# Gated linear attention in a two-layer decoder trunk: one score product per level for both 128-token blocks, and a new order of the gate rows

## The chip, the cores and the metric

One core of a Trainium2 chip runs the whole program in one launch. The metric is device time in microseconds (us). The time of the kernel before is the median of three runs. TensorE does matrix products, VectorE (DVE) and ScalarE (ACT) elementwise work, GpSimd (POOL) simple elementwise work, SyncE (SP) issues the transfers.

## The reference, cut to what matters

A batch of one with 256 tokens, 16 learned meta tokens ahead of them (272 rows), width 2048, passes two layers: gated linear attention (GLA) and a squared-ReLU MLP, then sliding-window attention and another MLP. The change lies in the GLA:

```python
q, k, v, g, r = split(xn @ w_in)                       # 4 heads, 256 key columns each
gk = log_sigmoid(r @ w_gate_up + b_gate) / 16          # a decay per key column and token
# per chunk of 64 tokens:
b = cumsum(gk)                                         # within the chunk
decay = exp(where(causal, b_i - b_j, -inf))
attn[i, j] = sum_d q[i, d] * k[j, d] * decay[i, j, d]
o = attn @ v + (q * exp(b)) @ S
S = S * exp(b_last) + (k * exp(b_last - b))^T @ v
```

The decay lies inside the sum over d, so attn isn't one matrix product of q and k.

## The kernel before

Everything is held transposed: features on the 128 partitions, tokens along the free axis. All big products are f32 made of three passes of a rounded type: `split_weight` (L84) makes of every 128x1024 half of a weight a rounded `hi` on ScalarE (L87) and the remainder `lo` on VectorE (L89), and `passes` (L99) issues, for each of 8 pieces, hi x hi, hi x lo and lo x hi (L110 to L112). A product (`product`, L114) thus has two halves of 24 matmuls; each needs its hi, and from its third matmul on its lo. `hi` and `lo` have three buffers each, `raw` four or more. The Tile scheduler, which goes by estimates of its own, orders each engine's queue from the dependencies; only the prologue (L265) fixes the order of TensorE, ScalarE and VectorE by hand, and other ready instructions may still be put between.

The prologue makes the normed input, the gate's low-rank rows `rr` and the first four key products. Then come the other key products (L316), the gate rows (L326: a small matmul `ps_z`, then abs, exp and ln on ScalarE, a minimum, a subtraction and a scan on VectorE, which give the running sums of the log decay `B`), eight query products (L339, ending in L341) and sixteen value products (`v_tile`, L361: the product, a scaling L364, three transposes `pt`).

Between the value products run the scores, a generator of steps (`scores`, L385), once for each pair of heads. A chunk's causal square is cut into levels s = 32, 16, ..., 1: in each block of 2s tokens the second s attend to the first s, and with the reference point at the end of the first s the decay splits into two factors of which neither grows. Per level: two GpSimd subtractions `E` (L411, L412), one exponential (L414), a product with the keys in place (L416) and one with the queries into `QL` (L417), which holds only the second halves, 64 columns per 128-token block. Then for each of the two blocks, two heads and two column groups one product `ps_l`: keys of the block as weights (128 columns), 64 query columns moving. VectorE masks the result (L423) and adds it, strided, into the scores `AT` (L426). The diagonal has its own products `ps_d` (L403, L404). After the levels: `QE` and `KD` carry the decays between chunks (L430 to L438); `ps_c` (L446) links the two chunks of a block, `ps_x` one block to the other, `ps_m` the meta tokens. `mix` (L513) multiplies the scores with the values.

Of the kernel before, what the change touches and what calls it, by code (L numbers as in the profile page):

```python
# [62 lines left out]
def trunk(ctx: ExitStack, tc: tile.TileContext, a: dict, out: bass.AP):  # L63
# [138 lines left out]
    def load(name, shape):  # L202
        t = const.tile(shape, F32, name=name)
        nc.sync.dma_start(t, a[name])
        return t
# [7 lines left out]
    with ExitStack() as gla:  # L213
# [109 lines left out]
        nc.gpsimd.memset(reset[:, 0:1], 0.0)  # L323
        nc.gpsimd.memset(reset[:, NM:L:CH], 0.0)
        B = bp.tile([P, 8, L], F32, tag="B", name="B")
        for f in range(8):  # L326
            ps = aux.tile([P, 512], F32, tag="aux", name="ps_z")
            nc.tensor.matmul(ps[:, :L], wgs[:, f * P:(f + 1) * P], rr, start=True, stop=True)
            e = tp.tile([P, L], F32, tag="t1", bufs=4, name="ge")
            nc.scalar.activation(e, ps[:, :L], AF.Abs, bias=bg[:, f:f + 1])  # L330
            lz = tp.tile([P, L], F32, tag="t2", bufs=4, name="gl")
            nc.vector.tensor_scalar(lz, ps[:, :L], bg[:, f:f + 1], 0.0, ALU.add, ALU.min)
            nc.scalar.activation(e, e, AF.Exp, scale=-1.0)
            nc.scalar.activation(e, e, AF.Ln, bias=1.0)
            nc.vector.tensor_sub(lz, lz, e)
            nc.vector.tensor_tensor_scan(B[:, f], reset, lz, 0.0, ALU.mult, ALU.add)

        Q = bp.tile([P, 8, L], F32, tag="Q", name="Q")
        for m in range(8):  # L339
            ps, = product(a["w_in"][m], xs)  # L340
            nc.vector.scalar_tensor_tensor(Q[:, m], ps, QS, rs, ALU.mult, ALU.mult)  # L341
# [43 lines left out]
        def scores(hp):  # L385
# [7 lines left out]
            def head_products(dst, n, lhs, rhs):  # L393

                for g in range(G):
                    for c in range(2):
                        t = 2 * g + c
                        nc.tensor.matmul(dst(g), lhs(t), rhs(t), start=(c == 0), stop=(c == 1))

            ps = aux.tile([P, 512], F32, tag="aux", name="ps_d")  # L400
            for jt in range(2):
                js = slice(jt * P, (jt + 1) * P)
                head_products(lambda g: ps[:, (jt * G + g) * P:(jt * G + g + 1) * P], P, lambda t: Kx[:, t, js], lambda t: Qx[:, t, js])  # L403
            nc.vector.tensor_mul(A_.rearrange("p g j i -> p j g i"), ps.rearrange("p (j g i) -> p j g i", j=2, g=G), ident[:, None, None, :].broadcast_to([P, 2, G, P]))  # L404
            yield
            for li, s in enumerate(LEVELS):
                n = SEQ // (2 * s)
                v = lambda t: t.rearrange("p f (n two s) -> p f n two s", two=2, s=s)
                E = bp.tile([P, F, SEQ], F32, tag="E", bufs=2, name="E")
                ref = v(Bx)[:, :, :, 0, s - 1:s].broadcast_to([P, F, n, s])  # L410
# [4 lines left out]
                QL = bp.tile([P, F, P], F32, tag="QL", bufs=2, name="QL")  # L415
                nc.vector.tensor_mul(v(E)[:, :, :, 0, :], v(E)[:, :, :, 0, :], v(Kx)[:, :, :, 0, :])  # L416
                nc.vector.tensor_mul(QL.rearrange("p f (n s) -> p f n s", s=s), v(E)[:, :, :, 1, :], v(Qx)[:, :, :, 1, :])  # L417
                yield
                ps = aux.tile([P, 512], F32, tag="aux", name="ps_l")
                for jt in range(2):  # L420
                    head_products(lambda g: ps[:, (jt * G + g) * CH:(jt * G + g + 1) * CH], CH, lambda t: E[:, t, jt * P:(jt + 1) * P], lambda t: QL[:, t, jt * CH:(jt + 1) * CH])
                psm = bp.tile([P, 2 * G * CH], F32, tag="psm", bufs=2, name="psm")
                nc.vector.tensor_mul(psm.rearrange("p (g i) -> p g i", i=CH), ps[:, :2 * G * CH].rearrange("p (g i) -> p g i", i=CH), lmask[:, None, li, :].broadcast_to([P, 2 * G, CH]))  # L423
                for jt in range(2):
                    dst = A_[:, :, jt].rearrange("p g (n two s) -> p g n two s", two=2, s=s)[:, :, :, 1, :]
                    nc.vector.tensor_add(dst, dst, psm[:, jt * G * CH:(jt + 1) * G * CH].rearrange("p (g n s) -> p g n s", g=G, s=s))  # L426
                yield

            Bc = Bx.rearrange("p f (c s) -> p f c s", s=CH)
# [4 lines left out]
            nc.vector.tensor_sub(KD[:, :, NM:].rearrange("p f (c s) -> p f c s", s=CH), Bc[:, :, :, CH - 1:CH].broadcast_to([P, F, NC, CH]), Bc)  # L434
            nc.vector.tensor_sub(KD[:, :, :NM], B_[:, :, NM - 1:NM].broadcast_to([P, F, NM]), B_[:, :, :NM])
            yield
            nc.scalar.activation(KD, KD, AF.Exp, scale=GATE)
            nc.vector.tensor_mul(KD, KD, K_)  # L438
# [3 lines left out]
            yield  # L442

            ps = aux.tile([P, 512], F32, tag="aux", name="ps_c")
            for jt in range(2):
                head_products(lambda g: ps[:CH, (jt * G + g) * CH:(jt * G + g + 1) * CH], CH, lambda t: KDx[:, t, jt * P:jt * P + CH], lambda t: QE[:, t, jt * P + CH:(jt + 1) * P])  # L446
            for jt in range(2):
                nc.vector.tensor_copy(A_[:CH, :, jt, CH:], ps[:CH, jt * G * CH:(jt + 1) * G * CH].rearrange("p (g i) -> p g i", i=CH))
# [23 lines left out]
            for li, s in enumerate(MLEVELS):  # L472
                n = NM // (2 * s)
                v = lambda t: t.rearrange("p f (n two s) -> p f n two s", two=2, s=s)
                ref = v(Bm)[:, :, :, 0, s - 1:s].broadcast_to([P, F, n, s])
                kv5 = v(K5[:, :, li])
                nc.vector.tensor_sub(kv5[:, :, :, 0, :], ref, v(Bm)[:, :, :, 0, :])
# [419 lines left out]
```

## Time and profile before

| | us |
|---|---|
| median of three runs (2210.8 to 2212.07) | 2211.91 |
| the profiled execution | 2212.41 |
| its span, first to last instruction | 2210.6 |
| TensorE busy | 2189.8 |
| VectorE busy | 1362.0 |
| ScalarE busy | 1066.9 |
| GpSimd busy | 237.0 |

The profiled execution is 0.5 us above the median, and 1.8 us of it lie outside the span. In a row of a timeline stand the start, the busy time, the engine, the source line, what is written and read, the shape, the count, and in brackets how long the engine sat idle just before and what ended that. In rows that group instructions the first number is the sum of busy times in us and the second the mean of one in ns. Matmuls are pipelined: one of 128x272 is busy 0.29 us, while the next starts 0.125 us after it, so prices on TensorE are read from start to start. The query products end at 117 us, the value products run from there to 256 us, the MLP and the second layer fill the rest and aren't touched.

### The profile page before, as it was taken

Reading aid. Unit: us, or ns where it says so; the run is one execution under the profiler, and the core shown is the slowest. Engines: PE = TensorE matmul, PEld = TensorE weight load, DVE = VectorE, ACT = ScalarE, POOL = GpSimd, SP = SyncE. Lnnn points to the kernel's source line nnn. Section 1 sums busy time; section 2 is a strip of 40 time slices with the busy share of each in tenths; the row PEclk is TensorE's granted clock in tenths of the full one; section 3 lists DMA queues with packets and bytes.
Section 4 is the critical chain, followed back from the end, with each engine's and each line's share of the span. In section 5 each row is a group of like instructions: output and inputs, shape, how many; then the busy total and the mean of one; then the engine's idle time right before and its main releaser. Section 6 shows DMA issues by size and latency. Waiting matters only on the chain. (4 is left out here: it accounts for less than half of the span.)

```text
span 2210.6 us, 38682 instructions
## 1 busy us (share of the span) xinstructions
PE 2189.8 (99%) x15796; PEld 2079.0 (94%) x15796; DVE 1362.0 (62%) x1941; ACT 1066.9 (48%) x1672; POOL 237.0 (11%) x248
## 2 busy tenths in 40 slices
PE   9999999999999999999999999999999999999997
PEld 9999999999999999999999999988888888888886
DVE  6768676665445545544556666686656655656665
ACT  5544455444334434433444568655435534534543
POOL 0112143310000000000013121060000000000022
PEclk9999999999999999999999999999999999999999
DMA  6443445565555555555554554466555555555552
GB/s 226 161 136 118 133 157 164 173 214 177 172 178 175 172 177 176 173 177 176 172 178 156 164 181 141 134 217 195 189 190 191 187 190 189 189 190 191 189 184 94
DMA packets 107393, 383.80 MB, mean 174 GB/s; under 512 B 13136, under 2 KB 14160, under 8 KB 107216
## 3 DMA queue, kind: packets, MB, share of 16 engines
q1 hardware_dynamic: 105056, 378.34, 52.2%
q0 software_dynamic: 1152, 2.38, 0.4%
q8 instruction: 123, 2.02, 0.4%
q10 hardware_dynamic: 1008, 0.63, 0.1%
q14 instruction: 54, 0.44, 0.1%
HBM read 376.82 MB, written 2.10 MB: 171 GB/s over the span
## 5 line engine op out<-in xcount | busy, mean ns | idle before, releaser
L87 ACT CAST hi<-raw 128x1024 fp32r<-128x1024 f32 x711 | 745.2, 1049 | 1038.9 <-PE ps L111 571.9
L89 DVE TENSOR_TENSOR lo<-raw,hi 128x1024 fp32r<-128x1024 f32 x711 | 878.4, 1236 | 597.0 <-ACT hi L87 589.8
L112 PE MATMUL ps<-x,lo 128*128 128x272 f32 (+1 forms) x2112 | 609.6, 289 | 4.4 <-DVE lo L89 4.2
L110 PE MATMUL ps<-x,hi 128*128 128x272 f32 (+1 forms) x2112 | 610.6, 289 | 0.5 <-ACT hi L275 0.3
L111 PE MATMUL ps<-x,hi 128*128 128x272 f32 (+1 forms) x2112 | 608.4, 288 | 0.3 <-DVE x L151 0.2
L112 PEld LDWEIGHTS ps<-x,lo 128*128 128x128 f32 x2112 | 397.2, 188 | 6.0 <-DVE lo L89 5.3
L111 PEld LDWEIGHTS ps<-x,hi 128*128 128x128 f32 x2112 | 401.4, 190 | 1.0 <-DVE x L151 0.9
L110 PEld LDWEIGHTS ps<-x,hi 128*128 128x128 f32 x2112 | 397.7, 188 | 3.7 <-issue 0.7
L107 PE MATMUL ps<-x,hi 128*128 128x512 f32 x1024 | 357.1, 392 | 0.0
L107 PE MATMUL ps<-hid,hi 128*128 128x512 f32 x1024 | 356.6, 392 | 0.0
L110 PE MATMUL ps<-hid,hi 128*128 128x272 f32 x1024 | 295.4, 289 | 0.0
L112 PE MATMUL ps<-hid,lo 128*128 128x272 f32 x1024 | 295.4, 289 | 0.0
L111 PE MATMUL ps<-hid,hi 128*128 128x272 f32 x1024 | 294.9, 288 | 0.0
L108 PE MATMUL ps<-x,lo 128*128 128x256 f32 x1024 | 287.6, 281 | 0.0
L108 PE MATMUL ps<-hid,lo 128*128 128x256 f32 x1024 | 287.1, 281 | 0.0
L107 PEld LDWEIGHTS ps<-x,hi 128*128 128x128 f32 x1024 | 192.0, 188 | 42.9
L107 PEld LDWEIGHTS ps<-hid,hi 128*128 128x128 f32 x1024 | 191.8, 188 | 42.6
L111 PEld LDWEIGHTS ps<-hid,hi 128*128 128x128 f32 x1024 | 194.8, 190 | 0.0
L108 PEld LDWEIGHTS ps<-hid,lo 128*128 128x128 f32 x1024 | 193.2, 189 | 0.3
L108 PEld LDWEIGHTS ps<-x,lo 128*128 128x128 f32 x1024 | 193.2, 189 | 0.1
L110 PEld LDWEIGHTS ps<-hid,hi 128*128 128x128 f32 x1024 | 192.4, 188 | 0.0
L112 PEld LDWEIGHTS ps<-hid,lo 128*128 128x128 f32 x1024 | 192.4, 188 | 0.0
(218 smaller groups left out, 2063.6 us busy)
## 6 DMA issues: line engine op xcount, KB each, us to landing
raw<-in_w_up SPq DMA_DIRECT2D x256, 512.0 KB, 3.4
raw<-in_w_down SPq DMA_DIRECT2D x256, 512.0 KB, 3.4
raw<-in_w_in SPq DMA_DIRECT2D x95, 512.0 KB, 3.3
raw<-in_w_out_a SPq DMA_DIRECT2D x32, 512.0 KB, 3.3
raw<-in_w_q SPq DMA_DIRECT2D x32, 512.0 KB, 3.9
raw<-in_w_out_b SPq DMA_DIRECT2D x32, 512.0 KB, 3.3
raw<-in_w_kv SPq DMA_DIRECT2D x8, 512.0 KB, 3.3
sw<-qt POOLq DMA_DIRECT2D x32, 64.0 KB, 2.4
```

The lines of the kernel that those rows point to most:

```text
L87: nc.scalar.copy(hi, raw)
L89: nc.vector.tensor_sub(lo, raw, hi.bitcast(F32))
L107: nc.tensor.matmul(ps[:, :2 * n], wh, x.both, start=begin, stop=False)
L108: nc.tensor.matmul(ps[:, n:2 * n], wl, x.hi, start=False, stop=end)
L110: nc.tensor.matmul(ps[:, :n], wh, x.hi, start=begin, stop=False)
L111: nc.tensor.matmul(ps[:, :n], wh, x.lo, start=False, stop=False)
L112: nc.tensor.matmul(ps[:, :n], wl, x.hi, start=False, stop=end)
```

## The change

**Levels.** Both blocks share one product: keys of the first block and queries of the second are the weights, queries of the first and keys of the second move, all 128 columns wide. A tile `W` holds for the first block its decayed keys at the first halves and, at the second halves, the second block's decayed queries, and the other way round. The result holds two triangles: the first block's scores above the diagonal, the second block's, transposed, below. Masked, it is added to `both`; at the end one transpose per head turns it, `above` cuts each triangle out, and it is added to the diagonal in `AT`. The decay difference is one VectorE subtraction (L424) in place of two on GpSimd, with the sign turned in the first of two exponentials (L426, L427). `ps_c` is written into `both` as well, for one block transposed, and copied by ScalarE (L469, L470).

**Masks.** `lmask` is now 128 wide: VectorE builds it from the loaded half mask, by a copy, a reduction of the identity and a subtraction per level (L355 to L359).

**Order.** A gate row is issued ahead of each query product, and the decay differences are tied behind the last query product on VectorE (`issue_after`).

```diff
-        for f in range(8):
+        def log_gate(f):
             ps = aux.tile([P, 512], F32, tag="aux", name="ps_z")
...
         for m in range(8):
+            log_gate(m)
             ps, = product(a["w_in"][m], xs)
-            nc.vector.scalar_tensor_tensor(Q[:, m], ps, QS, rs, ALU.mult, ALU.mult)
+            queries_done = nc.vector.scalar_tensor_tensor(Q[:, m], ps, QS, rs, ALU.mult, ALU.mult)
...
-        lmask = load("lmask", [P, len(LEVELS), CH])
+        half_mask = bp.tile([P, len(LEVELS), CH], F32, tag="W", bufs=2, name="half_mask")
+        nc.sync.dma_start(half_mask, a["lmask"])
...
+            nc.vector.tensor_reduce(block, ident.rearrange("p (n t) -> p n t", n=n), AX.X, ALU.add)
...
+            nc.vector.tensor_copy(m4[:, :, 1], hm)
+            nc.vector.tensor_sub(m4[:, :, 0], block[:, :, None].broadcast_to([P, n, s]), hm)
...
-                nc.gpsimd.tensor_sub(v(E)[:, :, :, 0, :], ref, v(Bx)[:, :, :, 0, :])
-                nc.gpsimd.tensor_sub(v(E)[:, :, :, 1, :], v(Bx)[:, :, :, 1, :], ref)
+                with tc.issue_after(queries_done.ins):
+                    nc.vector.tensor_sub(w(E), w(Bx), v(Bx)[:, :, :, 0, s - 1:s].broadcast_to([P, F, n, 2 * s]))
                 yield
-                nc.scalar.activation(E, E, AF.Exp, scale=GATE)
+                nc.scalar.activation(v(E)[:, :, :, 0, :], v(E)[:, :, :, 0, :], AF.Exp, scale=-GATE)
+                nc.scalar.activation(v(E)[:, :, :, 1, :], v(E)[:, :, :, 1, :], AF.Exp, scale=GATE)
+                W = bp.tile([P, F, SEQ], F32, tag="W", bufs=2, name="W")
+                nc.vector.tensor_mul(v(W)[:, :, :, 0, :], v(E)[:, :, :, 0, :], v(Kx)[:, :, :, 0, :])
+                for jt in range(2):
+                    js, other = slice(jt * P, (jt + 1) * P), slice((1 - jt) * P, (2 - jt) * P)
+                    nc.vector.tensor_mul(v(W[:, :, other])[:, :, :, 1, :], v(E[:, :, js])[:, :, :, 1, :], v(Qx[:, :, js])[:, :, :, 1, :])
...
-                for jt in range(2):
-                    head_products(lambda g: ps[:, (jt * G + g) * CH:(jt * G + g + 1) * CH], CH, lambda t: E[:, t, jt * P:(jt + 1) * P], lambda t: QL[:, t, jt * CH:(jt + 1) * CH])
+                head_products(lambda g: ps[:, g * P:(g + 1) * P], P, lambda t: W[:, t, :P], lambda t: W[:, t, P:])
...
+                    nc.vector.tensor_mul(psm, ps3, mask)
+                    nc.vector.tensor_add(both, both, psm)
...
+            for g in range(G):
+                nc.tensor.transpose(pt[:, g * P:(g + 1) * P], both[:, g], ident)
```

The scheduler's order shows it at three places of VectorE's queue. In these rows L89 is a weight remainder; the lines of the kernel after are its own.

First, among the gate rows and query products. Before, between the first and the second finished query product (L332, L335 and L336 are the gate rows, L434 and L435 the decays `KD`, L341 a finished query product):

```order
L89 TENSOR_TENSOR lo<-raw,hi 128x1024
L332 TENSOR_SCALAR gl<-ps_z,b_gate 128x272 x2
L335 TENSOR_TENSOR gl<-gl,ge 128x272
L434 TENSOR_TENSOR KD<-B 128x4x256
L435 TENSOR_TENSOR KD<-B 128x4x16
L335 TENSOR_TENSOR gl<-gl,ge 128x272
L89 TENSOR_TENSOR lo<-raw,hi 128x1024
L459 TENSOR_TENSOR D_1937<-DC 128x4
L336 SCALAR_TENSOR_TENSOR B<-reset,gl 128x272
L335 TENSOR_TENSOR gl<-gl,ge 128x272 x2
L341 SCALAR_TENSOR_TENSOR Q<-ps,rstd 128x272
```

After, at the first two query products (L333, L336 and L337 are the gate row, L343 the query product):

```order
L333 TENSOR_SCALAR gl<-ps_z,b_gate 128x272
L336 TENSOR_TENSOR gl<-gl,ge 128x272
L337 SCALAR_TENSOR_TENSOR B<-reset,gl 128x272
L89 TENSOR_TENSOR lo<-raw,hi 128x1024
L343 SCALAR_TENSOR_TENSOR Q<-ps,rstd 128x272
L89 TENSOR_TENSOR lo<-raw,hi 128x1024
L333 TENSOR_SCALAR gl<-ps_z,b_gate 128x272
L336 TENSOR_TENSOR gl<-gl,ge 128x272
L337 SCALAR_TENSOR_TENSOR B<-reset,gl 128x272
L89 TENSOR_TENSOR lo<-raw,hi 128x1024
```

Three instructions of one gate row and one finished query product now stand between remainders; KD and the work on E are gone from here.

Second, in the prologue. Before, from the third quarter of the input pieces (L151) to the remainder after the first sum of squares (L255; L313 prepares the gate weights):

```order
L151 SCALAR_TENSOR_TENSOR x<-h,gains,x 128x272 x4
L89 TENSOR_TENSOR lo<-raw,hi 128x1024
L151 SCALAR_TENSOR_TENSOR x<-h,gains,x 128x272 x4
L313 TENSOR_TENSOR wgs<-wg,wgs 32x1024
L89 TENSOR_TENSOR lo<-raw,hi 128x1024
L255 TENSOR_TENSOR squares<-squares 128x2176
L89 TENSOR_TENSOR lo<-raw,hi 128x1024
```

After, the last four L151 with the mask work among them (L358 copies, L355 reductions, L359 differences):

```order
L151 SCALAR_TENSOR_TENSOR x<-h,gains,x 128x272 x2
L358 COPY lmask<-half_mask 128x2x32
L151 SCALAR_TENSOR_TENSOR x<-h,gains,x 128x272
L359 TENSOR_TENSOR lmask<-block,half_mask 128x2x32
L358 COPY lmask<-half_mask 128x4x16
L358 COPY lmask<-half_mask 128x8x8
L358 COPY lmask<-half_mask 128x16x4
L358 COPY lmask<-half_mask 128x32x2
L151 SCALAR_TENSOR_TENSOR x<-h,gains,x 128x272
L358 COPY lmask<-half_mask 128x64
L355 TENSOR_REDUCE block<-ident 128x4
L359 TENSOR_TENSOR lmask<-block,half_mask 128x4x16
```

The mask copies have moved in among the last input pieces; two more reductions stand before the next remainder, one of them after L313, and five more mask instructions between the remainders up to L305.

Third, behind the last query product. Before (L364 scales a value product, L375, L404, L423 and L426 belong to the first scores):

```order
L341 SCALAR_TENSOR_TENSOR Q<-ps,rstd 128x272
L89 TENSOR_TENSOR lo<-raw,hi 128x1024 x2
L364 TENSOR_TENSOR vt<-ps,rstd 128x272
L89 TENSOR_TENSOR lo<-raw,hi 128x1024 x2
L375 TENSOR_TENSOR VM<-pt,VM 16x128
L404 TENSOR_TENSOR AT<-ps_d,ident 128x2x2x128
L423 TENSOR_TENSOR psm<-ps_l,lmask 128x256
L426 TENSOR_TENSOR AT<-AT,psm 128x2x2x32 x2
L364 TENSOR_TENSOR vt<-ps,rstd 128x272
L416 TENSOR_TENSOR E<-E,K 128x64x8
L417 TENSOR_TENSOR QL<-E,Q 128x512
```

After (L424 the decay differences, L451 and L452 KD, L429 and L432 the factors in W, L380 scales a value product):

```order
L343 SCALAR_TENSOR_TENSOR Q<-ps,rstd 128x272
L424 TENSOR_TENSOR E<-B 128x1024 x2
L451 TENSOR_TENSOR KD<-B 128x4x256
L452 TENSOR_TENSOR KD<-B 128x4x16
L89 TENSOR_TENSOR lo<-raw,hi 128x1024
L429 TENSOR_TENSOR W<-E,K 128x16x32
L432 TENSOR_TENSOR W<-E,Q 128x4x2x32 x2
L89 TENSOR_TENSOR lo<-raw,hi 128x1024
L429 TENSOR_TENSOR W<-E,K 128x32x16
L432 TENSOR_TENSOR W<-E,Q 128x4x4x16 x2
L380 TENSOR_TENSOR vt<-ps,rstd 128x272
L455 TENSOR_TENSOR KD<-KD,K 128x1088
```

Between the remainders, where the queue had nothing but remainders and a scaling, the differences and factors of the first two levels now stand.

More of the change, by code (lines that the diff above doesn't have):

```diff
@@ L398, in head_products @@
                         nc.tensor.matmul(dst(g), lhs(t), rhs(t), start=(c == 0), stop=(c == 1))
-            ps = aux.tile([P, 512], F32, tag="aux", name="ps_d")
-            for jt in range(2):
[L402 to L405, printed above, removed]
+            both = bp.tile([P, G, P], F32, tag="both", bufs=1, name="both")
             for li, s in enumerate(LEVELS):
@@ L422, in scores @@
[L422 to L426, printed above, removed]
+                head_products(lambda g: ps[:, g * P:(g + 1) * P], P, lambda t: W[:, t, :P], lambda t: W[:, t, P:])
@@ L427, in scores @@
+                ps3, mask = ps[:, :G * P].rearrange("p (g i) -> p g i", g=G), lmask[:, None, li, :].broadcast_to([P, G, P])
+                if li == 0:
+                    nc.vector.tensor_mul(both, ps3, mask)
+                else:
+                    psm = bp.tile([P, G, P], F32, tag="psm", bufs=2, name="psm")
+                    nc.vector.tensor_mul(psm, ps3, mask)
+                    nc.vector.tensor_add(both, both, psm)
                 yield
@@ L476, in scores @@
                 kv5 = v(K5[:, :, li])
-                nc.vector.tensor_sub(kv5[:, :, :, 0, :], ref, v(Bm)[:, :, :, 0, :])
+                with tc.issue_after(queries_done.ins):
+                    nc.vector.tensor_sub(kv5[:, :, :, 0, :], ref, v(Bm)[:, :, :, 0, :])
                 nc.vector.tensor_sub(kv5[:, :, :, 1, :], v(Bm)[:, :, :, 1, :], ref)
```

43 lines of the change are left out of this document (33 added, 10 removed).

## The prediction

> **What bounds the kernel now.** I read the page first, then the busy times by stretch, then the waits of TensorE one by one in its timeline, and last the prices of single instructions.
>
> ```profile
> PE 2189.8 (99%) x15796; PEld 2079.0 (94%) x15796; DVE 1362.0 (62%) x1941; ACT 1066.9 (48%) x1672; POOL 237.0 (11%) x248
> ...
> 63.00:117.00 54.00, 50.65 (x400) 50.00 (x399) 41.21 (x59) 28.45 (x46) 6.17 (x4) 1.00 0.48 156
> 117.00:256.00 139.00, 139.00 (x1152) 137.41 (x1151) 104.33 (x185) 61.02 (x115) 21.95 (x20) 1.00 0.39 126
> ```
>
> TensorE is the bound: 99% of the span, and without a gap in 117 to 256 us, where the value products and all scores run (columns: PE, PEld, DVE, ACT, POOL). A TensorE instruction taken out there is worth its whole issue interval. In 63 to 117 us, gate rows and query products, it idles 3.35 us:
>
> ```profile
> 26.38 0.39 PE L112 MATMUL ps<-x,lo 128*128 128x272 f32 x1 [0.69 <-DVE lo L89]
> ...
> 39.51 0.36 PE L110 MATMUL ps<-x,hi 128*128 128x272 f32 x1 [0.18 <-DVE K L305]
> ...
> 82.03 0.39 PE L112 MATMUL ps<-x,lo 128*128 128x272 f32 x1 [1.62 <-DVE lo L89]
> ...
> 86.12 0.39 PE L112 MATMUL ps<-x,lo 128*128 128x272 f32 x1 [1.09 <-DVE lo L89]
> ...
> 90.29 0.40 PE L112 MATMUL ps<-x,lo 128*128 128x272 f32 x1 [0.64 <-DVE lo L89]
> ```
>
> All those waits are for VectorE's weight remainders (lo), made strictly in queue order. So two questions decide: how much TensorE work goes, and whether each lo stays early enough.
>
> **TensorE's work.** A matmul of plain f32 shows as two records, which cost their distance from start to start:
>
> ```profile
> 126.69 0.27 PE L370 MATMUL pt<-ident,metas 128*80 128x128 f32 x1
> 126.80 1.50 PE L398 MATMUL ps_d<-Q,K 128*128 128x128 f32 x12
> 128.14 1.90 PE L398 MATMUL ps_l<-QL,E 128*128 128x64 f32 x16
> 129.84 0.37 PE L110 MATMUL ps<-x,hi 128*128 128x272 f32 x1
> ...
> L398 PE MATMUL ps_l<-QL,E x192: 217/275/275, 128.1 to 226.1; 128*128 128x64 f32 x192
> ...
> 170.45 0.91 PE L398 MATMUL ps_c<-QE,KD 128*64 128x64 f32 x12
> 171.29 0.31 PE L370 MATMUL pt<-ident,metas 128*80 128x128 f32 x1
> ...
> 256.83 0.60 PE L520 MATMUL ps_o<-AT,V 128*128 128x256 f32 x2
> 257.26 0.38 PE L521 MATMUL ps_o<-AT,V 128*128 128x128 f32 x2
> ```
>
> Sixteen ps_l records of 64 columns take 1.70 us, 0.106 each; twelve ps_d records of 128 columns take 1.34, 0.112 each. So 64 columns cost nearly what 128 do. Before: 192 x 0.106 = 20.4 us. After: half the products with 128 columns, 96 x 0.112 = 10.8. Four transposes of the joint sums are new, 0.11 each by L370: 0.4. ps_c keeps 32 records, 0.070 each; half of them now use the other 64 output rows, and if such neighbours overlapped fully, 16 x 0.070 = 1.1 would go too; I take nothing and keep 1.1 for the low end. ps_d moves and costs the same. Sum: 9.2 us less, on the path.
>
> The Trainium skill, "TensorE: Matmul & The Clock Gate", section "Back-to-back issue gap", gives N/2.4 + 2.5 ns for an isolated matmul of N moving columns, and itself says that this counts too little at small N in a stream with weight loads. By the formula the term would be 192 x 29 ns against 96 x 56 ns, a gain of 0.2 us and not 9.6; the trace's 106 ns for 64 columns speaks against it here.
>
> **The gate rows.** One gate row now stands ahead of each query product, and the score work that had slipped in between (L434, L435, L416, L438) is held behind the last query.
>
> ```profile
> L336 DVE TENSOR_TENSOR_SCAN B<-reset,gl 128x272 f32<-128x272 f32 x8 | 5.4, 704 | 0.0
> L335 DVE TENSOR_TENSOR gl<-gl,ge 128x272 f32<-128x272 f32 x8 | 4.2, 550 | 0.3 <-ACT ge L334 0.3
> L332 DVE TENSOR_SCALAR gl<-ps_z,b_gate 128x272 f32<-128x272 f32 x8 | 3.6, 489 | 0.0
> ...
> 111.16 0.44 DVE L341 SCALAR_TENSOR_TENSOR Q<-ps,rstd 128x272 f32<-128x272 f32 x1 [0.83 <-PE ps L112]
> 117.18 0.44 DVE L341 SCALAR_TENSOR_TENSOR Q<-ps,rstd 128x272 f32<-128x272 f32 x1 [0.83 <-PE ps L112]
> ```
>
> Per product VectorE then has two lo (1.22 each), one gate row (0.70 + 0.55 + 0.49) and one L341 (0.44): 4.6 us of 6.02. The three stalls go: 3.35 us less. Were a row late, lo of the next half would still have a whole half product, 3.0 us, in hand.
>
> **The masks.** The full masks are now built on VectorE inside the prologue, from a load that came at the same place in SyncE's queue.
>
> ```profile
> 17.83 0.33 SPq L204 DMA_DIRECT2D lmask<-in_lmask  x1
> ...
> lmask<-in_lmask SPq DMA_DIRECT2D x1, 192.0 KB, 3.3
> ...
> norm_out<-in_norm_out SPq DMA_DIRECT2D x1, 2.0 KB, 5.1
> ...
> 4.83 0.28 DVE L356 TENSOR_REDUCE fold<-ident 80x16 f32<-80x80 f32 x1
> ...
> 20.14 1.73 DVE L151 SCALAR_TENSOR_TENSOR x<-h,gains,x 128x272 fp32r<-128x272 f32 x4
> 23.85 1.22 DVE L313 TENSOR_TENSOR wgs<-wg,wgs 32x1024 fp32r<-32x1024 f32 x1 [1.98 <-ACT wgs L312]
> 25.09 1.23 DVE L89 TENSOR_TENSOR lo<-raw,hi 128x1024 fp32r<-128x1024 f32 x1
> ...
> 37.31 1.23 DVE L89 TENSOR_TENSOR lo<-raw,hi 128x1024 fp32r<-128x1024 f32 x1 [0.43 <-ACT hi L87]
> ...
> 38.92 1.48 DVE L305 TENSOR_TENSOR K<-ps,rstd 128x272 f32<-128x272 f32 x4
> ...
> L484 DVE COPY Q<-Q x2: 183/185/187, 95.0 to 193.9; 128x64 f32<-128x64 f32 x2
> ```
>
> VectorE instructions overlap by 0.08 us. A mask copy (like L484) is 0.11 behind another, a difference some 0.14, a reduction of 128 columns some 0.30 (an estimate, above L356's 0.28 for 80 columns less the overlap). The load lands at 17.83 + 3.3 = 21.1, when VectorE arrives after two of the four L151. Ahead of the fourth then stand five copies and one difference, 0.7: that x comes 0.8 later, and TensorE with it, but this eats the 0.69 it waits at 26.38. The rest is nearly hidden under the 1.98 that VectorE waits ahead of L313; one reduction behind L313 is not: first lo, and TensorE, 0.3 later. One difference ahead of the next lo: 0.44 in all. Two reductions and two differences more, 0.9, stand ahead of L305, whose result the matmul at 39.51 already waits for; VectorE's own wait of 0.43 at 37.31 takes some of it up. So I take 0.9 more in all, between 0.44 and the full 1.3; the bounds are 0, if all hides, and 2.7, if the load takes 5.1 us like norm_out's and everything behind it comes 1.8 later.
>
> **The value products.** With no work for GpSimd there, VectorE gets the differences for the decays.
>
> ```profile
> L89 DVE TENSOR_TENSOR lo<-raw,hi 128x1024 fp32r<-128x1024 f32 x33 | 40.3, 1221 | 18.8 <-ACT hi L87 18.7
> L426 DVE TENSOR_TENSOR AT<-AT,psm 128x128 f32<-128x128 f32 x24 | 16.5, 727 | 0.3
> L364 DVE TENSOR_TENSOR vt<-ps,rstd 128x272 f32<-128x272 f32 x16 | 7.0, 437 | 6.3 <-PE ps L112 6.2
> L416 DVE TENSOR_TENSOR E<-E,K 128x512 f32<-128x512 f32 x10 | 6.8, 683 | 0.1
> L417 DVE TENSOR_TENSOR QL<-E,Q 128x512 f32<-128x512 f32 x10 | 6.8, 681 | 0.0
> L460 DVE TENSOR_TENSOR QE<-QE,DC 128x256 f32<-128x256 f32 x2 | 0.8, 418 | 0.0
> ...
> L438 DVE TENSOR_TENSOR KD<-KD,K 128x1088 f32<-128x1088 f32 x1 | 1.3, 1291 | 0.0
> ...
> L434 DVE TENSOR_TENSOR KD<-B x2: 1219/1658/2098, 76.5 to 178.8; 128x1024 f32<-128x1024 f32 x2
> ```
>
> Less the overlap, 24 L426 (15.6 us) and 10 L417 (6.0) leave. Twelve decay differences come (like L434 alone, 1.14: 13.7), 24 half products of queries (like L460, 0.34: 8.2), two more of L416 (1.2), 18 sums and final products (0.34: 6.1) and KD of the first half (2.5). Net 10 more: 104.3 becomes 114 us, TensorE's 139.0 becomes 129.8. Enough in sum; but a lo waits its turn in the queue, and E, W and lo have only two or three buffers. So I walk the queue where it is fullest, in us after the last matmul of the queries. Behind L343 (0.2 after it, 0.36 long) stand two differences and KD (3 x 1.14 + 0.14) and then the lo of the third half product, 1.22: done at 5.3. It is needed in the third half's third matmul, at 2 x 3.01 + 0.25 = 6.3. Then follow three factors of W (0.60 + 2 x 0.34) and a lo (1.14): 7.7, with more than a half product in hand. Then three factors again (1.28), a scaling (0.36), KD's product (1.2), a third difference (1.14) and a lo (1.22): 12.9. TensorE reaches that one after 100 big matmuls (100 x 0.125 = 12.5) and, which the scheduler put ahead of it, three transposes and four score products (11 x 0.11 = 1.2): 13.7. The lo after it has 1.5 in hand by the same walk, later ones 3 and more, since the first half of the scores is then well ahead. I take no stall; the thinnest margins are 1.0 and 0.8.
>
> What else moves lies on engines with room: ScalarE's exponentials come in halves (24 of 512 columns) and it copies ps_c, with 61 us of 139 used so far; each query product's remainders are cast as before. GpSimd makes `above` in the prologue and then has nothing until the mixing, where it works as before. A transpose waits for the last sum in `both` and for ScalarE's copies of ps_c; the eight ps_d products stand ahead of it, 16 x 0.112 = 1.8 us, which covers those two. If that cover were gone, TensorE would wait twice, once per half of the scores, for about a copy's time each.
>
> **Sum.** 9.2 + 3.35 - 0.9 = 11.6 us less. The profiled execution took 2212.4, so 2200.8; from the median of the runs shown, 2211.9, it is 2200.3. I say 2200.5. From no change a measurement of this kernel can tell about 0.2%, 4.4 us.
>
> **Rivals.** *Late remainders among the first value products.* If a decay difference costs L434's dear price, 2.10, as it did beside GpSimd, the two walks end 3 x 0.88 = 2.6 and 4 x 0.88 = 3.5 later: TensorE waits 1.6 at the first place, 1.1 more at the second and some 0.3 at the next; 3.0 us back, 2203.8. For it: thin margins. Against it: the other L434 took 1.22, and GpSimd has nothing there any more. The Trainium skill, "SBUF — State Buffer", section "Who interferes with whom", calls GpSimd and VectorE rivals for one exclusively locked port pair; by that rule, and the two prices of L434 agree with it, the dear price can't come back. Chance 0.10.
>
> *A matmul's price follows its columns.* L520's 256 columns take 0.43 / 2 = 0.215; in proportion 64 take 0.054 and 128 take 0.108, so 192 and 96 records cost the same 10.4. Only stalls and masks would count: 2212.4 - 3.35 + 0.9 + 0.4 = 2210.4, no change. The formula above is of this kind. The 0.106 speaks against it. Chance 0.04.
>
> *Slower: VectorE becomes the bound of the value products.* Its 114 us must pass TensorE's 129.8 by more than the 11.6 gained: 27 us more, from 2.3 us extra on each of twelve differences (3.5 each). At 4.0 it would be 12 x 2.8 = 33 more, 17 over TensorE's, and 2218. The dearest row is 2.10. Chance 0.03.
>
> My forecast has the other 0.83. The range: low end 2197.0, if masks hide (0.9) and ps_c overlaps (1.1), less the 1.3 us by which the runs differ; high end 2206.5, with the late load (1.8), the late remainders (3.0) and that scatter. Chances: faster 0.83 + 0.10 = 0.93, same 0.04, slower 0.03.
>
> **What would show it.** Right: 96 ps_l records about 0.11 apart; no TensorE wait for L89 between the first gate row and the last query; about 1 us more of waits before 41 us; none, or under 1 us, in the first four value products. Wrong: ps_l records 0.2 apart; decay differences over 1.3 us; TensorE's busy share in the value stage under 99%.

## The result, and the profile after

The kernel after takes 2197.68 us (median of four runs, 2197.28 to 2197.83), the one before in the same job 2211.55 (four runs, 2210.8 to 2212.07): a ratio of 0.9937, 95% interval 0.992 to 0.9954. That is 13.9 us less, where the forecast had 11.6.

First the engines' busy times on the page of the kernel after:

```profile
PE 2177.3 (99%) x15704; PEld 2066.9 (94%) x15704; DVE 1367.0 (62%) x1973; ACT 1071.8 (49%) x1688; POOL 210.8 (10%) x226
```

TensorE has 92 records fewer (96 of ps_l gone, 4 transposes come) and is still busy for 99%: the bound is the same, the work is less. To see where the time went I cut both traces at the same instructions of TensorE: the start of the last matmul ahead of the first gate row, of the first behind the last query product, and of the first behind the last value product. Busy times between these cuts (the stretch, its length, then PE, PEld, DVE, ACT, POOL), before and after:

```profile
63.56:116.98 53.42, 50.07 (x395) 49.42 (x394) 41.16 (x58) 28.45 (x46) 6.17 (x4) 1.00 0.48 158
116.98:252.47 135.49, 135.49 (x1124) 133.90 (x1123) 102.41 (x183) 59.42 (x112) 21.95 (x20) 1.00 0.39 126
```

```profile
64.85:114.15 49.30, 49.30 (x396) 49.30 (x394) 36.13 (x51) 27.06 (x42) 0.00 (x0) 1.00 0.51 171
114.15:238.84 124.69, 124.69 (x1032) 123.07 (x1030) 108.17 (x204) 65.54 (x132) 0.00 (x0) 1.00 0.41 136
```

The prologue ends 1.3 us later (64.85 for 63.56), the query stage takes 49.3 us instead of 53.4, and the value stage 124.7 instead of 135.5: 1.3 - 4.1 - 10.8 = -13.6. (The value products of the kernel before end at 252.5 us; the 256 us named ahead of the prediction reach into the mixing, whose first product starts at 255.7.) From there on the distance stays at 13.65 up to 1242 us of the kernel before. The other 0.9 by which the two profiled runs differ lies in the second layer's attention, which the change doesn't touch; the medians differ by 13.9.

TensorE is now busy without a gap in both stages. VectorE's share of the value stage rises from 76% (102.4 of 135.5) to 87%, and TensorE doesn't wait for it there.

The score products of the kernel after, in the timeline of TensorE:

```profile
141.68 1.50 PE L414 MATMUL ps_l<-W 128*128 128x128 f32 x12
142.93 0.37 PE L111 MATMUL ps<-x,hi 128*128 128x272 f32 x1
...
162.76 0.22 PE L468 MATMUL ps_c<-QE,KD 128*64 128x64 f32 x1
162.77 0.22 PE L468 MATMUL ps_c<-KD,QE 128*64 128x64 f32 x1
162.82 0.22 PE L468 MATMUL ps_c<-QE,KD 128*64 128x64 f32 x1
```

Twelve ps_l records of 128 moving columns take 1.25 us, 0.104 each; one inside a run takes 0.112, as one of 64 columns did before. From each start to the next start, all 96 sum to 10.23 us, the 192 before to 20.50. The second thing to see: ps_c records now come in pairs that start some 0.006 apart, one pair every 0.059. The 32 of them take 1.38 us instead of 2.29.

The prologue, VectorE's timeline and then TensorE's:

```profile
21.58 0.20 DVE L358 COPY lmask<-half_mask 128x64 f32<-128x64 f32 x1 [0.45 <-DMA half_mask<-in_lmask]
...
23.16 0.28 DVE L355 TENSOR_REDUCE block<-ident 128x4 f32<-128x128 f32 x1
...
40.21 1.49 DVE L305 TENSOR_TENSOR K<-ps,rstd 128x272 f32<-128x272 f32 x4
```

```profile
23.20 0.49 PE L234 MATMUL ps_r<-x,wrs 128*96 128x272 f32 x2 [0.60 <-DVE x L151]
...
40.80 0.36 PE L110 MATMUL ps<-x,hi 128*128 128x272 f32 x1 [0.66 <-DVE K L305]
```

The load comes where the working had it (21.58 for 21.1), part of the masks hides under VectorE's old wait ahead of L313, and the rest pushes L305 from 38.92 to 40.21 and TensorE's wait for it from 0.18 to 0.66.

### The profile page after: what moved, and what is told of

Read it like the earlier page. It is cut to its first block, busy times and chain, and to the rows that moved or that the text cites. A ratio compares the mean times of both kernels' runs of the same rounds, so it can differ in the third digit from the quotient of the medians.

```text
span 2196.1 us, 38512 instructions
## 1 busy us (share of the span) xinstructions
PE 2177.3 (99%) x15704; PEld 2066.9 (94%) x15704; DVE 1367.0 (62%) x1973; ACT 1071.8 (49%) x1688; POOL 210.8 (10%) x226
## 4 chain that ended last, share of the span: by engine, by line
PE 98%; DMA 1%; DVE 1%; ACT 0%; DVEq 0%; issue 0%; SPq 0%; ACTq 0%
PE ps L107 23%; PE ps L110 20%; PE ps L112 20%; PE ps L111 20%; PE ps L108 12%; PE s L737 1%; DMA raw<-in_w_in 1%; PE ps_pv L761 1%; PE pt L750 0%; PE ps_l L414 0%; PE ps_o L558 0%; PE ps_d L414 0%; DMA half_mask<-in_lmask 0%; PE ps_ssq L172 0%; PE ps_o L559 0%; PE ps_m L414 0%
## 5 line engine op out<-in xcount | busy, mean ns | idle before, releaser
L89 DVE TENSOR_TENSOR lo<-raw,hi 128x1024 fp32r<-128x1024 f32 x711 | 879.3, 1237 | 583.4 <-ACT hi L87 576.1
```

What stands on the lines that cost most here:

```text
L89: nc.vector.tensor_sub(lo, raw, hi.bitcast(F32))
```

## The experiments

Two theories on the query stage. **A**, the prediction's: TensorE stalled because score work stood between gate rows and remainders in VectorE's queue, and the new order cured it. **B**: it stalled because VectorE became slow there beside GpSimd's decay differences, and taking GpSimd out cured it. In the kernel before, VectorE's rows in that stretch and GpSimd's:

```profile
76.47 2.10 DVE L434 TENSOR_TENSOR KD<-B 128x1024 f32<-128x1024 f32 x1
78.49 1.06 DVE L435 TENSOR_TENSOR KD<-B 128x64 f32<-128x64 f32 x1
79.47 1.36 DVE L335 TENSOR_TENSOR gl<-gl,ge 128x272 f32<-128x272 f32 x1
80.76 1.21 DVE L89 TENSOR_TENSOR lo<-raw,hi 128x1024 fp32r<-128x1024 f32 x1
```

```profile
74.37 1.88 POOL L411 TENSOR_TENSOR E<-B 128x512 f32<-128x512 f32 x1 [34.89 <-DMA raw<-in_w_in]
76.21 1.27 POOL L412 TENSOR_TENSOR E<-B 128x512 f32<-128x512 f32 x1
77.44 2.02 POOL L411 TENSOR_TENSOR E<-B 128x512 f32<-128x512 f32 x1
79.43 1.11 POOL L412 TENSOR_TENSOR E<-B 128x512 f32<-128x512 f32 x1
```

Three VectorE instructions beside the last three of GpSimd's four cost 4.52 us; elsewhere the same three cost 1.22, 0.22 and 0.44. The remainder at 80.76, for which TensorE waits 1.62, stands right behind them, 2.6 us later than by those prices.

All runs in one table: time, ratio to the kernel before on the same chip, and from each profile, by the cuts above, where the prologue ends and how long the query and the value stage are. The experiments ran on several chips; the kernel before took 2211.09 to 2211.55 us on them, so a difference of under 0.5 us between two rows says nothing.

| kernel | us | ratio to before, 95% | prologue ends | queries | values |
|---|---|---|---|---|---|
| before | 2211.55 | | 63.56 | 53.4 | 135.5 |
| after | 2197.68 | 0.9937 (0.992 to 0.9954) | 64.85 | 49.3 | 124.7 |
| gates first | 2197.75 | 0.9937 (0.9923 to 0.9952) | 64.19 | 49.3 | 124.7 |
| no hold | 2197.44 | 0.9936 (0.992 to 0.9953) | 64.62 | 49.4 | 124.6 |
| masks loaded | 2196.25 | 0.9931 (0.9916 to 0.9946) | 63.35 | 49.3 | 124.7 |
| ps_c apart | 2198.09 | 0.9939 (0.9924 to 0.9954) | 64.62 | 49.3 | 125.2 |
| old order | 2200.04 | 0.995 (0.9935 to 0.9965) | 64.46 | 51.7 | 124.6 |
| order alone | 2207.22 | 0.9981 (0.9972 to 0.999) | 63.70 | 49.3 | 135.5 |
| differences on GpSimd | 2197.62 | 0.9939 (0.9922 to 0.9955) | 64.48 | 49.3 | 124.7 |
| two halves | 2207.77 | 0.9986 (0.9977 to 0.9996) | 64.38 | 49.3 | 135.1 |
| before, no reads | 2207.25 | 0.9982 (0.9973 to 0.9992) | 63.07 | 49.5 | 135.3 |
| differences twice | 2198.51 | 0.9942 (0.9927 to 0.9957) | 64.18 | 49.3 | 119.9 |
| differences three times | 2204.14 | 0.9968 (0.9955 to 0.998) | 64.47 | 49.3 | 114.3 |

(In the last two rows the scheduler moved score work behind the last value product, so their value stage is shorter and a later one longer; the paragraph on them measures up to a later matmul.)

**Gates first, and no hold.** The two halves of the new order, each undone alone.

```diff
         for m in range(8):
             log_gate(m)
+        for m in range(8):
             ps, = product(a["w_in"][m], xs)
```

> The kernel after, with all eight gate rows issued ahead of the first query product as before; the score work stays tied behind the last query. Theory A, the stalls of the query stage came from score work and GpSimd among the remainders: TensorE waits less than 1 us there and the time rises by less than 1 us. Rival B, they came from the block of gate rows itself: the three stalls are back, 3 to 4 us more.

```diff
-                with tc.issue_after(queries_done.ins):
-                    nc.vector.tensor_sub(w(E), ...)
+                nc.vector.tensor_sub(w(E), ...)
...
```

(the same for the differences of KD and K5)

> The kernel after, without the ties of score work to the last query product; gate rows stay one per query product. Theory A: VectorE's differences move in among the queries, remainders come late there, 1 to 4 us more. Rival B: less than 0.5 us of change.

Both take what the kernel after takes, and their query stage is 49.3 and 49.4 us long. The second goes against what A expected: from 87.3 us a decay difference and both parts of KD (1.23, 1.22 and 0.22) stand between VectorE's remainders again, and TensorE waits for none of them. The placing of the gate rows alone isn't needed, and the hold alone isn't either.

**Old order.** Both halves undone at once; the only thing that is still new ahead of the value products is that the differences are VectorE's.

> The changed kernel with both halves of the new order undone: all eight gate rows ahead of the first query product, and no hold on the differences, so that score work stands again between gate rows and remainders in VectorE's queue (three decay differences, KD and W now, all on VectorE). GpSimd still has nothing there. Theory A (the three stalls came from this order): 3 to 4 us are back between the first gate row and the last query, 2201 to 2202. Rival B (they came from VectorE instructions that grew dear beside GpSimd's differences, L434 2.10, L435 1.06 and L335 1.36 us, some 2.7 us more than their usual prices): under 0.5 us, 2197.7 give or take 0.5, and L336's sums stay under 0.8 us each.

It takes 2200.04, 2.4 us more than the kernel after, all of it in the query stage: 51.7. That is between the two. A stall of 1.20 is back at the old place and one of 0.60 at 92.25, but the rows ahead of the first have their usual prices:

```profile
77.34 2.35 DVE L424 TENSOR_TENSOR E<-B 128x1024 f32<-128x1024 f32 x2
79.61 1.22 DVE L450 TENSOR_TENSOR KD<-B 128x1024 f32<-128x1024 f32 x1
80.74 0.43 DVE L336 TENSOR_TENSOR gl<-gl,ge 128x272 f32<-128x272 f32 x1
81.09 0.22 DVE L451 TENSOR_TENSOR KD<-B 128x64 f32<-128x64 f32 x1
81.23 1.22 DVE L89 TENSOR_TENSOR lo<-raw,hi 128x1024 fp32r<-128x1024 f32 x1
```

```profile
82.50 0.39 PE L112 MATMUL ps<-x,lo 128*128 128x272 f32 x1 [1.20 <-DVE lo L89]
```

Two decay differences, 2.35 us, stand now where 2.6 us of waiting beside GpSimd stood. So this run alone doesn't decide between A and B: it takes the slowness away and puts as much work in its place.

**Order alone.** The other way about: the kernel before, with `log_gate(m)` ahead of each query product and the hold on KD and K5; GpSimd keeps its differences, the products stay as they were.

> The kernel before with the new order alone: gate rows one ahead of each query product, VectorE's differences for KD and K5 held behind the last query; the decay differences stay on GpSimd and the score products stay as they were. Theory A: the stalls go, 4 us less than the kernel before, 2207.5. Rival B: GpSimd still works beside the queries and makes VectorE dear, so TensorE still waits there: 2209 to 2211.5. With A and B both at work the order alone also suffices, since VectorE then has 1.4 us of slack per product: 2207.5, with dear VectorE rows beside GpSimd's.

2207.22: all of the stalls' 4.1 us are gone (49.3 us, with no gap of TensorE), though GpSimd still works there and VectorE still pays for it. Its timeline, VectorE and then GpSimd:

```profile
86.55 2.07 DVE L89 TENSOR_TENSOR lo<-raw,hi 128x1024 fp32r<-128x1024 f32 x1 [0.19 <-ACT hi L87]
88.55 1.04 DVE L462 TENSOR_TENSOR D<-DC 128x4 f32<-128x4 f32 x1
```

```profile
86.51 1.04 POOL L413 TENSOR_TENSOR E<-B 128x512 f32<-128x512 f32 x1 [46.89 <-DVE B L337]
87.50 2.06 POOL L414 TENSOR_TENSOR E<-B 128x512 f32<-128x512 f32 x1
```

So the new order is enough by itself, as A has it: the remainder at 86.55 is 0.85 dearer, and TensorE doesn't notice.

**Before, no reads.** What A leaves open is whether the old order stalled by itself. GpSimd's 24 subtractions become fills with a constant, so this kernel leaves out the decay differences.

```diff
-                nc.gpsimd.tensor_sub(v(E)[:, :, :, 0, :], ref, v(Bx)[:, :, :, 0, :])
-                nc.gpsimd.tensor_sub(v(E)[:, :, :, 1, :], v(Bx)[:, :, :, 1, :], ref)
+                nc.gpsimd.memset(v(E)[:, :, :, 0, :], -1.0)
+                nc.gpsimd.memset(v(E)[:, :, :, 1, :], -1.0)
```

> The kernel before with GpSimd's 24 subtractions replaced by fills of the same tiles with a constant: the decay differences are left out, so the scores are not the reference's; every other instruction stays, and GpSimd reads nothing there. The old order stands: ahead of the remainder for which TensorE waited 1.62 us come L434, L435, L335 as before, and one L416 (0.60) more, put there by the scheduler. Theory B (dear VectorE rows beside GpSimd made the stalls): 2.10 + 1.06 + 1.36 go back to about 1.22 + 0.22 + 0.44, 2.6 us earlier, so 1.62 + 0.60 - 2.6 leaves no stall there, the query stage takes 49.3 to 50.3 instead of 53.4, and the time is 2207.4 to 2208.5. Theory A (the order itself): the stage keeps 2.4 us of the 4.1 or more, 2209.8 to 2211.5.

2207.25, a query stage of 49.5, and no wait of TensorE there. VectorE's timeline from the first fill to the old place, and the two fills:

```profile
70.54 0.78 DVE L335 TENSOR_TENSOR gl<-gl,ge 128x272 f32<-128x272 f32 x2
...
75.19 1.21 DVE L434 TENSOR_TENSOR KD<-B 128x1024 f32<-128x1024 f32 x1
76.32 0.22 DVE L435 TENSOR_TENSOR KD<-B 128x64 f32<-128x64 f32 x1
76.46 0.68 DVE L416 TENSOR_TENSOR E<-E,K 128x512 f32<-128x512 f32 x1
...
78.17 1.22 DVE L89 TENSOR_TENSOR lo<-raw,hi 128x1024 fp32r<-128x1024 f32 x1
```

```profile
70.33 0.52 POOL L411 MEMSET E<- 128x512 f32 x1 [31.34 <-PE ps_z L328]
70.79 0.53 POOL L412 MEMSET E<- 128x512 f32 x1
```

The rows are cheap, those beside the fills too (two L335 in 0.78), and the old order with its score work among the gate rows doesn't stall, even with one product more ahead of the remainder. So B names what made the kernel before stall, and A a cure: the old order has room for the score work, but not for some 2.5 us more, whether these are waits beside GpSimd (2.6, before) or the differences themselves (2.35, old order); the new one has room for either.

**Differences on GpSimd.** The twelve decay differences go back, one subtraction each, and the hold on them goes.

```diff
-                with tc.issue_after(queries_done.ins):
-                    nc.vector.tensor_sub(w(E), ...)
+                nc.gpsimd.tensor_sub(w(E), ...)
```

> The changed kernel with its twelve decay differences on GpSimd instead of VectorE, one instruction each, not held behind the last query. VectorE loses 12 x 1.14 = 13.7 us in the value products. If TensorE sets the pace there and margins only have to be positive: 0, 2197.7 give or take 0.5. If instructions beside GpSimd grow dear as L434 did before (2.10 instead of 1.22), rows of 1.6 us or more stand beside GpSimd's in VectorE's timeline, and TensorE waits for remainders again: 1 to 4 us, 2199 to 2202.

2197.62, the time of the kernel after. The dear rows are there; the first of VectorE and of GpSimd:

```profile
87.35 2.97 DVE L89 TENSOR_TENSOR lo<-raw,hi 128x1024 fp32r<-128x1024 f32 x1 [0.19 <-ACT hi L87]
```

```profile
87.30 1.94 POOL L423 TENSOR_TENSOR E<-B 128x1024 f32<-128x1024 f32 x1 [46.90 <-DVE B L337]
```

A remainder that costs 1.22 elsewhere takes 2.97 when it starts 0.05 us behind GpSimd's 1.94, as if it stood still until GpSimd was done. This agrees with the Trainium skill, "SBUF — State Buffer", section "Who interferes with whom", by which a VectorE instruction with two inputs contends with a GpSimd instruction that reads, over ports that are locked for one of them. Yet both stages keep their length: TensorE waits for no remainder there, and once, 0.20 us, for a scaled value product. With gate rows among the query products, taking the differences off GpSimd is worth nothing that these runs can tell.

**Two halves.** Each level product issued as two of 64 moving columns: the same columns and weights, twice the instructions.

```diff
-                head_products(lambda g: ps[:, g * P:(g + 1) * P], P, ..., lambda t: W[:, t, P:])
+                for h0 in (0, CH):
+                    head_products(lambda g: ps[:, g * P + h0:g * P + h0 + CH], CH, ..., lambda t: W[:, t, P + h0:P + h0 + CH])
```

> The changed kernel with each level product issued as two products of 64 moving columns: the same columns, twice the instructions (192 ps_l records instead of 96), half of them reloading the same weights. If the price goes by the instruction (0.106 us a record, whatever the columns): 96 x 0.106 = 10.2 us more, 2207.9. If it goes by the columns (0.054 for 64): no change, 2197.7 give or take 0.5, and records 0.054 apart.

2207.77, 10.1 us more, and the value stage 10.4 longer. With 128 weight columns and up to 128 moving ones, the price goes by the instruction. Its timeline:

```profile
126.49 1.67 PE L414 MATMUL ps_l<-W 128*128 128x64 f32 x14
127.97 0.37 PE L110 MATMUL ps<-x,hi 128*128 128x272 f32 x1
```

Fourteen records of 64 columns take 1.48 us, 0.106 each, in the kernel after's own surroundings. This is the term on which the forecast stood, shown by itself.

**ps_c apart.** The products of ps_c issued block by block, so that neighbours write the same output rows.

```diff
-            for g in range(G):
-                for c in range(2):
-                    t = 2 * g + c
-                    for jt, rows, l, r in (...):
+            for jt, rows, l, r in (...):
+                for g in range(G):
+                    for c in range(2):
+                        t = 2 * g + c
```

> The kernel after, with the ps_c products of one block all ahead of those of the other, so that neighbours write the same 64 output rows. Theory: the overlap of neighbours with different output rows is gone, ps_c records cost 0.070 us again and not 0.043, 0.9 us more. Rival: the price came from elsewhere, no change.

2198.09, 0.4 more, which single runs can't tell (2197.33 to 2198.45 here, 2197.28 to 2197.83 for the kernel after); the value stage grows by 0.5, not by the 0.9 expected. The scheduler mixed the two blocks again in part, and that shows both prices in one place. TensorE's timeline of this kernel:

```profile
211.90 0.50 PE L468 MATMUL ps_c<-QE,KD 128*64 128x64 f32 x5
212.19 0.27 PE L468 MATMUL ps_c<-KD,QE 128*64 128x64 f32 x1
212.24 0.22 PE L468 MATMUL ps_c<-QE,KD 128*64 128x64 f32 x1
212.30 0.22 PE L468 MATMUL ps_c<-KD,QE 128*64 128x64 f32 x1
212.30 0.22 PE L468 MATMUL ps_c<-QE,KD 128*64 128x64 f32 x1
```

The five of one block that start at 211.90 stand 0.058 apart from the second on; at 212.30 two of different blocks start together, and the next pair follows 0.058 later, the time of one alone. The 32 records take 1.89 us in all, between 2.29 (never alternating) and 1.38 (always).

**Masks loaded.** The full masks come from memory, 384 KB instead of 192, and VectorE builds nothing.

```diff
-        half_mask = bp.tile(...)
-        nc.sync.dma_start(half_mask, a["lmask"])
         lmask = vp.tile([P, len(LEVELS), P], F32, name="lmask")
+        nc.sync.dma_start(lmask, a["lmask"])
-        for li, s in enumerate(LEVELS):
-            ...
```

> The kernel after, with the full masks loaded (384 KB in place of 192) and nothing built on VectorE. If the masks on VectorE cost what the trace suggests, the query stage begins 1.0 to 1.5 us earlier and the time is that much shorter, about 2196.4. Rival: the longer load delays the weights behind it in the same queue and takes it back, no change or slower.

2196.25, 1.4 us less than the kernel after by the medians; its prologue ends at 63.35. It is the fastest kernel of this study; its four runs (2195.4 to 2196.99, on another chip) all lie below those of the kernel after, by an amount about as large as their own scatter.

**Differences twice and three times.** How far is VectorE from being the bound? Each decay difference is computed again, with the same result.

```diff
                 with tc.issue_after(queries_done.ins):
-                    nc.vector.tensor_sub(w(E), ...)
+                    for twice in range(2):
+                        nc.vector.tensor_sub(w(E), ...)
```

> The changed kernel with each of its twelve decay differences computed twice, one behind the other (same result): 12 x 1.14 = 13.7 us more on VectorE, 108.2 + 13.7 = 121.9 of the value stage's 124.7. How near is VectorE to being the bound? Walk of the queue (the scheduler puts only the first pair and KD ahead of the third lo, the second pair behind it): lo done at 5.3, 8.7 and 11.4 us after the last query against a need at 6.3, 9.3 and 12.3, so no stall in the first halves; in the stretch after that, with 97% of VectorE taken, 0 to 2 us: 2198 to 2200. Rival (the margins of 1.0 and 0.8 are used up by any extra difference): 2.6 us and more, 2200.3 or above, with waits for L89 in the first four value products.

> The changed kernel with each of its twelve decay differences computed three times: 27.4 us more on VectorE, 108.2 + 27.4 = 135.6 us against TensorE's 124.7 in the value stage. If VectorE becomes the bound there: 10.9 us more at least, 2208.6, and up to 4 more where it waits itself, 2208.6 to 2213, with VectorE near 100% of the stage and TensorE waiting for lo of L89. If VectorE's work lay beside TensorE's whatever its sum: 2198 to 2202.

Twice costs 0.8 us, and behind the prologue TensorE waits for no remainder of L89: the extra 13.7 us lie beside its work (its one new wait is for GpSimd's sum of squares in the mixing). Three times costs 6.5, less than the 10.9 expected. The busy times of that kernel, from the first gate row to well behind the value products, and those of the kernel after between the same two matmuls:

```profile
64.47:330.02 265.55, 262.48 (x2090) 258.99 (x2088) 232.11 (x374) 141.21 (x266) 31.42 (x33) 0.99 0.44 144
```

```profile
64.85:325.22 260.37, 260.37 (x2089) 257.63 (x2088) 205.13 (x351) 144.68 (x271) 33.20 (x35) 1.00 0.45 148
```

VectorE takes 27.0 us more, of which 5.2 reach the end of this stretch; TensorE waits twice for a remainder in it, 0.22 and 1.93 us. The expectation took the value stage's length for fixed; the scheduler gave the late scores more room by moving them behind the value products (the last ps_l record starts at 249.0 us instead of 211.7). VectorE's work goes over into time only bit by bit.

## Why the prediction was right, and where its sizes were off

The direction, the main mechanism (fewer score products, each at nearly the old price) and the size held: 2200.5 said, 2197.68 measured, inside the range but only 0.7 above its low end. Two of the terms behind 11.6 were too small, and the cause given for one of them was wrong for the kernel before.

*TensorE's work, 9.2 said, 10.8 measured.* The step "192 x 0.106 against 96 x 0.112" was right in what it says: a record costs 0.112 inside a run with 64 or 128 moving columns, and the two halves show it. Mis-sized were its ends. The 96 records took 10.23 and not 10.8, since the last of a run costs only some 0.03 where a big product follows, which the row of twelve, followed by other score products, didn't show. And of the step "I take nothing and keep 1.1 for the low end" for ps_c, 0.9 of the 1.1 came. The kernel before issues no such neighbours, so its trace couldn't show the overlap; the bound could be had from it, the choice within the bound couldn't. Together: 20.50 - 10.23 + 0.91 - 0.35 for the new transposes = 10.8. From start to start, what the last of a run saves can fall on its neighbour: the stage's big products take 0.5 us more than before, and its other small ones 0.5 less, which cancel here. So the gain at the ends is less certain than that of ps_c.

*The stalls, 3.35 said, 4.1 measured.* All three went, and the order alone does that. The change also took GpSimd's subtractions out, and that is enough as well (the fills); so the stalls' going is no evidence for the cause that the prediction gave, and the term came out by luck in that respect. Two steps were off. The smaller is the reading of the idle column as the whole loss. The matmuls around the first stall, in the kernel before:

```profile
80.13 0.28 PE L111 MATMUL ps<-x,hi 128*128 128x272 f32 x1
82.03 0.39 PE L112 MATMUL ps<-x,lo 128*128 128x272 f32 x1 [1.62 <-DVE lo L89]
82.26 0.29 PE L110 MATMUL ps<-x,hi 128*128 128x272 f32 x1
```

From start to start 1.90 and then 0.23 us pass where 0.125 each is usual: 1.88 lost for 1.62 idle. The idle time counts from the end of a record, and records overlap; a stall costs some 0.26 more than its idle time, three of them 0.8. The larger is the cause: "the score work that had slipped in between" was not too much in itself; L434, L435 and L335 were too dear. The prediction had L434's two prices in hand, but used them for a rival in the value products and not for the stalls.

*The masks, 0.9 said.* In the profiled run 1.3, but one run scatters. Nine profiles have the masks on VectorE (the kernel after and all its variants but *masks loaded*): their prologue ends between 64.18 and 64.85, on the mean at 64.47. The three with the kernel before's prologue end at 63.07, 63.56 and 63.70, on the mean at 63.44. The difference of the means is 1.0. The rows that it was made of came as worked out: the reductions at 0.28 to 0.29, the load in time, L305 late by 1.3.

*The value products, no stall.* The walk of VectorE's queue ended at 5.3 and 12.9 us behind the last query; in the trace the two remainders end 5.3 and 12.8 behind the cut at 114.15 (rows of the kernel after):

```profile
118.25 1.22 DVE L89 TENSOR_TENSOR lo<-raw,hi 128x1024 fp32r<-128x1024 f32 x1
...
124.61 1.22 DVE L424 TENSOR_TENSOR E<-B 128x1024 f32<-128x1024 f32 x1
125.75 1.22 DVE L89 TENSOR_TENSOR lo<-raw,hi 128x1024 fp32r<-128x1024 f32 x1
```

The decay differences cost 1.22, the cheap price, and TensorE has no gap in that stage. VectorE's work there rose by 5.8 us (102.4 to 108.2) and not by the 10 of the working, which left out, among others, the four copies of ps_c (1.1 us) that went to ScalarE.

The rivals: *late remainders* did not come, and the differences put on GpSimd show that even remainders of 2.97 us would have been in time in the query stage. *Price follows columns* is refuted by the two halves. *VectorE the bound* was to cost the whole gain at 27 us of extra work; with that much (three times) about half of the gain is left, 2204.14. The loss begins between 14 us (twice, +0.8) and 27 us (+6.5), and grows more slowly than the plain difference of the sums.

What stays open: the fills are not only free of reads but shorter too (0.52 us each for 1.1 to 2.0) and come earlier than the subtractions did, so that run shows that GpSimd's subtractions made VectorE dear, and not for certain that it is their reading that did. Why a ps_c record alone costs 0.058 and a pair hardly more was not taken further. And of the 0.9 us in the second layer's attention, all that can be said is that all twelve other profiles show 0.5 to 1.2 less there than that of the kernel before, the order-alone kernel's, which is the same there, 0.7: it belongs to that one profiled execution.

## What to carry to other kernels

On a core whose TensorE is busy for 99%, count small matmuls with 128 weight columns by the instruction and not by the moving columns: two products of 64 moving columns that can be had as one of 128 cost half as much that way, and products that fill only half the output rows are best issued alternating between the halves. A stall behind another engine's queue is one sum of work and of waits: look in the trace for instructions there that cost more than their like elsewhere, for here either slack (the new order) or quiet (no GpSimd beside it) ended the same stall, and the two gains don't add. Read the loss of a stall from start to start of the instructions, not from the idle column.

## What the runs showed of the hardware

TensorE's price of a plain f32 matmul record in these traces follows the larger of two column counts. With 128 weight columns and 64 moving: 0.112 us inside a run; 128 and 128: 0.112; 64 and 64: 0.058; and 0.215 for 128 and 256 (the row of L520 in the prediction). The Trainium skill, "TensorE: Matmul & The Clock Gate", section "LDWEIGHTS (loading the stationary operand)", gives P/1.2 ns for a load of P weight columns. Worked out from that, an estimate, 128 and 64 weight columns take 107 and 53 ns; the records of 64 moving columns, 112 and 58 ns, agree with it within 10%.

Two records that write different halves of the output rows, 64 weight columns each, overlapped almost wholly: a pair every 0.059 us, as much as one alone.

A VectorE subtraction of two inputs beside a GpSimd subtraction took 2.97 us instead of 1.22, and even L462 of the order-alone kernel, with 4 elements in each partition, took 1.04 there; its like in the kernel after, L496, takes 0.16. In the rows above these are waits for an instruction of GpSimd's that started earlier: L462 ends at 89.59, 0.03 behind GpSimd's, and the remainder of 2.97 us ends 1.08 behind GpSimd's end at 89.24. Started first, VectorE keeps its price and GpSimd waits. VectorE and GpSimd in the kernel with the differences on GpSimd:

```profile
99.24 1.22 DVE L89 TENSOR_TENSOR lo<-raw,hi 128x1024 fp32r<-128x1024 f32 x1
```

```profile
99.49 2.85 POOL L423 TENSOR_TENSOR E<-B 128x1024 f32<-128x1024 f32 x1 [3.96 <-DVE W L431]
```

GpSimd's 1.94 have become 2.85 here, 0.9 more, and VectorE's remainder was still running for 0.97 us when it started.
